# Hymba decoder layer on one core: K22 and KT4 activations in a right-hand pool of their own, the up product's pool 32 KiB lower

## The chip, the cores and the metric

The kernel runs on 1 core of one Trainium2 chip. The metric is the device time of one execution in microseconds; lower is better. Three executions of the kernel before took 2115.16, 2113.25 and 2115.39 us (median 2115.16). The profile comes from one more execution, which took 2114.84 us.

## What is computed

One decoder layer for 512 positions of width 2048 (float32): RMSNorm, an input projection, eight attention heads beside a 16-head SSM scan, an output projection added to x, and then the part that this change touches, the ConvGLU:

```python
x = x + jnp.concatenate([attn, ssm], axis=-1) @ w_out
h = rms_norm(x, norm2_w)
u = causal_dwconv(h @ w_up, ffn_conv_w, ffn_conv_b)
u_gate, u_val = jnp.split(u, 2, axis=-1)
return x + (jax.nn.silu(u_gate) * u_val) @ w_down
```

`w_up` is 2048 x 11264, `w_down` 5632 x 2048.

## The kernel before

**Two stages.** The first stage (to about 800 us) does everything up to and with the output projection, with helper functions whose instructions all stand under line 183. The second stage does the up and the down product. This change touches the second stage alone.

**The second stage.** Both products are done block by block with a 2 x 2 scheme of seven products (Strassen-Winograd): four weight quarters and four activation quarters are combined by sums into seven weight blocks and seven *kinds* of activations, `KT1, KT3, K11, KT2, K21, K22, KT4` (numbers 0 to 6, line 61). `groups` (lines 978 to 988) lists 44 groups of the up product and then 3 x 8 groups of the down product (passes over 7, 8 and 7 pairs of hidden blocks). Each group has seven items, `P1` to `P7`; `KIND` (line 63) says which kind each item uses: `P3` uses K22, `P4` uses KT4. Lines 997 to 999 set the order: P5 of a group, P3 of the group before, P1, P4 of the group before, P6, P2, P7.

**One item** ("slot") is lines 1285 to 1290: for each of n blocks (8 in the up product and the second pass, 7 in the first and third) two matmuls with the high half of the weights (`hi2`) against the high and the low half of the kind, and after them n matmuls with the low half of the weights (`lo2`) against the high half of the kind. So the weights of every matmul come from `hi2` or `lo2`, the moving operand (128 x 256) from a kind's tile `cmb0` to `cmb6`:

```python
pe.matmul(out, w, bk[:, 0, q, :], ...)
pe.matmul(out, w, bk[:, 1, q, :], ...)
...
pe.matmul(out, l[:, q * 128:(q + 1) * 128], bk[:, 0, q, :], ...)
```

The matmuls with the low half stand under line 1289 and are shown by the trace as one run of eight (or seven) per item.

**What feeds it.** SP loads the weights into `rawa` and `rawb`; DVE and POOL make the weight sums (lines 1013 to 1030); ACT makes `hi2` (line 1041) and DVE `lo2` (line 1050) some slots ahead. After an item, DVE or ACT takes its result out of PSUM (`up_after`, `down_after`). `events` and `after` hold what is issued at each slot; each engine works in the order of issue. The activations of a down pass come back from DRAM through `ld` tiles and are split into the kinds by `b_split` (lines 1096, 1097).

**Where tiles lie.** Pools are stacked from both ends of each partition's memory. From the near end: the constants, then, once the first stage's pools `w` and `ab` are closed, the pool `w2` (`lp`, line 970): `par2`, `rawb` x2, `rawa` x4, `acc_s` x2, `hi2` x3, `lo2` x2, and last `cmb5` (K22) and `cmb6` (KT4). From the far end: the pool `cmb` with `cmb0` to `cmb4`, written by `g_x2` during the output projection (lines 915 to 920), then `work2` (`xin` x5, `gx` x2, `sq`), which is closed at the start of the up product, and in its place the pool `up` (`ug`, `uv`, `ld`, `cP`, `tg`, `tv`, `gt`; line 1239), later `down`. A kind is 2 x 8 x 256 x 4 = 16,384 bytes per partition. By the order of allocation the bytes of each partition are:

| tile | bytes before | bytes after |
|---|---|---|
| first stage: `hi`, `lo` (weights) | 33,952 to 46,624 | same |
| first stage: `A`, `B` | 46,624 to 112,160 | same |
| first stage: `PTh`, `PTl`, `vh`, `vl` (attention) | 180,192 to 196,576 | same |
| `hi2`, `lo2` | 55,840 to 76,320 | same |
| `cmb5` (K22) | 76,320 to 92,704 | 114,656 to 131,040 |
| `cmb6` (KT4) | 92,704 to 109,088 | 131,040 to 147,424 |
| `up` | 110,432 to 147,424 | 77,664 to 114,656 |
| `work2` | 118,752 to 147,424 | same |
| `cmb0` to `cmb4` | 147,424 to 229,344 | same |

**The start of the up product.** K22 and KT4 are not made by `g_x2`. It stores their sums to DRAM (`xd`, line 921); `start_up` (line 1236) issues the first three `x_load`s, and `x_split` at the slots 2, 4, 5 and 6 (lines 1126 to 1136) writes K22 and KT4 from the `ld` tiles with ACT (line 1131) and DVE (line 1132). `P3` of the first group is slot 6, `P4` slot 8. A tile in a pool with `reuse_waits="tile"` waits for the last users of the older tiles that lay in its place.

Of the kernel before, what the change touches and what calls it, by code (L numbers as in the profile page):

```python
# [60 lines left out]
KT1, KT3, K11, KT2, K21, K22, KT4 = range(7)  # L61
# [126 lines left out]
def body(ctx, tc, xT, wi, wz, wo, wu, wd0, wd1, wd2, pp, pf, outT, dbg={}):  # L188
# [659 lines left out]
    p2 = {}  # L848

    def phase2():  # L850
        while gens:
            advance(True)
        work.close()
        cw.close()
        p2["cmb"] = ctx.enter_context(tc.tile_pool(name="cmb", bufs=1, side="right"))
        p2["kinds"] = [None] * 7
        for t in (KT1, KT3, K11, KT2, K21):
            p2["kinds"][t] = cmb_tile(t)
        p2["pool"] = work.enter_context(tc.tile_pool(name="work2", bufs=1, side="right"))
        p2["ssq"] = rbc  # L860

    def cmb_tile(t):

        pool = p2["cmb"] if t < K22 else p2["cmbl"]
        return pool.tile([128, 2, 8, 256], F32R, name="cmb%d" % t)

    x2d = [dram.tile([128, S], F32, name="x2d%d" % j) for j in range(NK)]
# [100 lines left out]
    ab.close()  # L968
    ve, se, pe, po, sy = nc.vector, nc.scalar, nc.tensor, nc.gpsimd, nc.sync
    lp = ctx.enter_context(tc.tile_pool(name="w2", bufs=1, reuse_waits="tile"))  # L970
    p2["cmbl"] = lp
    p2["par"] = lp.tile([128, NPF], F32, name="par2")
    sy.dma_start(p2["par"], pf)
    def side_tile(pool, shape, name, bufs=1):
# [113 lines left out]
    def b_split(k):  # L1088
        p, t, h = b_list[k]
        ph = [g for g in groups if g["ph"] == "down" and g["p"] == p][0]["kinds"]  # L1090
        m = PASSES[p][1] - 4 if h else 4
        if h == 0:
            ph[t] = cmb_tile(t)
        ld = lds.pop(0)
        hi, lo = (ph[t][:, x, 4 * h:4 * h + m, :] for x in range(2))
        se.activation(hi, ld[:, :m, :], AF.Copy)
        ve.tensor_tensor(lo, ld[:, :m, :], hi.bitcast(F32), op=OP.subtract)  # L1097
# [23 lines left out]
    def x_load(n):  # L1121
        if n < 4:
            x_ld.append(side_tile(box["pool"], [4, 256], "ld", 3))
            sy.dma_start(x_ld[n], xd[:, 4 * (n % 2):4 * (n % 2) + 4, n // 2, :])

    def x_split(n):
        t, h = (K22, KT4)[n // 2], n % 2
        if h == 0:
            up_kinds[t] = cmb_tile(t)
        o = up_kinds[t][:, :, 4 * h:4 * h + 4, :]  # L1130
        se.activation(o[:, 0], x_ld[n], AF.Copy)
        ve.tensor_tensor(o[:, 1], x_ld[n], o[:, 0].bitcast(F32), op=OP.subtract)
        x_load(n + 3)
# [102 lines left out]
    def start_up():  # L1236

        work.close()
        box["pool"] = up_stack.enter_context(tc.tile_pool(name="up", bufs=1, side="right", reuse_waits="tile"))
        box["depth"] = 3  # L1240
        for n in ("ug0", "uv0", "ug1", "uv1"):
            box[n] = box["pool"].tile([128, 516], F32, name=n)
            ve.memset(box[n][:, 0:2], 0.0)
        x_load(0), x_load(1), x_load(2)
# [21 lines left out]
    while gens:  # L1266
# [3 lines left out]
                                               reuse_waits="tile"))  # L1270
    step_slot(-2), step_slot(-1)
    for k, (gi, x) in enumerate(items):
        g = groups[gi]
        if x == "P5":
            g["X"] = box["ps"].tile([128, 512], F32, name="x")
        if x == "P2":
            g["Y"] = box["ps"].tile([128, 512], F32, name="y")
        out = g["Y"][:, :256] if x == "P2" else g["X"][:, 256:] if x in ("P5", "P3") else g["X"][:, :256]
        h, l = parts.pop(k)
        bk = g["kinds"][KIND[x]]  # L1280
        n = g["n"]
        fresh = x in ("P5", "P2")
        for part in ((range(n - 1), range(n - 1, n)) if k < 2 else (range(n),)):
            for q in part:
                w = h[:, q * 128:(q + 1) * 128]
                pe.matmul(out, w, bk[:, 0, q, :], start=fresh and q == 0, stop=False, skip_group_check=True)  # L1286
                pe.matmul(out, w, bk[:, 1, q, :], start=False, stop=False, skip_group_check=True)  # L1287
            for q in part:
                pe.matmul(out, l[:, q * 128:(q + 1) * 128], bk[:, 0, q, :], start=False, stop=q == n - 1,  # L1289
                          skip_group_check=True)  # L1290
        if k == 0:
            start_up()
        (up_after if g["ph"] == "up" else down_after)(g, x)
        step_slot(k)
# [23 lines left out]
```

## Time and profile before

| | |
|---|---|
| median of 3 executions | 2115.16 us (2113.25 to 2115.39) |
| the profiled execution | 2114.84 us |
| its span, first to last instruction | 2113.1 us |
| PE busy | 2073.9 us (98%) |
| DVE busy | 1583.5 us (75%) |
| ACT busy | 988.3 us (47%) |
| mean share of the DMA engines that is busy, second stage | some 40 to 80% |
| granted TensorE clock, mean | 0.998 |

The table stands for one profiled execution. PE is the bound of nearly the whole kernel, so a change is read from how closely its matmuls follow one another, and from the few places where it waits. In the chain of waits a run of matmuls of one line is merged into one piece, with its start, its length and its count; the distance between the starts of two such pieces is the time of one item.

### The profile page before, as it was taken

What the parts mean: (1) busy time and instruction counts of PE and PEld (TensorE: products, weight loads), DVE (VectorE), ACT (ScalarE), POOL (GpSimd) and SP (SyncE); (2) the same over time, 40 slices, a digit from 0 to 9 for tenths busy, and PEclk for the clock granted to TensorE, in tenths of its full rate; (3) what the DMA queues carried; (4) which work ended last, traced back from release to release, by engine and by line L of the source; (5) the groups of instructions that cost most, each with busy time, mean ns of one, the idle gap of its engine ahead of it and who ended that gap; (6) DMA issues with size and microseconds to landing.
All of it is one profiled execution on the core that took longest, in us unless ns stands there. A gap on an engine that the chain in (4) does not pass through costs nothing.

```text
span 2113.1 us, 37694 instructions
## 1 busy us (share of the span) xinstructions
PE 2073.9 (98%) x15366; PEld 1949.7 (92%) x15366; DVE 1583.5 (75%) x2251; ACT 988.3 (47%) x1433; POOL 207.9 (10%) x107
## 2 busy tenths in 40 slices
PE   9999999999999998999999999999999899999999
PEld 7888887888888878999999999999999899899999
DVE  6545555345555558999999999999999977977976
ACT  5433435244344435555555555555555534534532
POOL 0020000000000001111110111011111111101110
PEclk9999999999999999999999999999999999999999
DMA  5233222332225535445444444454455667856763
GB/s 194 75 115 91 71 75 76 99 101 80 80 70 172 165 129 188 158 141 189 160 156 165 170 168 155 157 183 158 142 188 201 215 215 242 274 184 231 260 201 120
DMA packets 114396, 328.18 MB, mean 155 GB/s; under 512 B 10736, under 2 KB 35120, under 8 KB 111408
## 3 DMA queue, kind: packets, MB, share of 16 engines
q1 hardware_dynamic: 114224, 325.78, 45.5%
q8 instruction: 120, 1.97, 0.4%
q14 instruction: 52, 0.43, 0.1%
HBM read 283.77 MB, written 41.98 MB: 154 GB/s over the span
## 4 chain that ended last, share of the span: by engine, by line
PE 88%; DVE 7%; issue 2%; ACT 1%; DMA 1%; SPq 0%; DVEq 0%; POOL 0%; ACTq 0%; POOLq 0%
PE acc L183 29%; PE x L1289 16%; PE x L1286 16%; PE x L1287 16%; PE sm L183 4%; PE y L1289 3%; PE y L1287 3%; PE y L1286 3%; DVE lo L1050 2%; DVE cmb L1097 1%; DVE lo L183 1%; DVE acc L1151 0%; DVE s L1024 0%; DMA raw<-wi 0%; DVE s L1030 0%
## 5 line engine op out<-in xcount | busy, mean ns | idle before, releaser
L1287 PE MATMUL x<-cmb,hi 128*128 128x256 f32 x3168 | 755.0, 279 | 12.5 <-DVE cmb L1097 10.9
L1286 PE MATMUL x<-cmb,hi 128*128 128x256 f32 x3168 | 755.8, 279 | 11.5 <-ACT cP L1166 5.4
L1287 PEld LDWEIGHTS x<-cmb,hi 128*128 128x128 f32 x3168 | 599.3, 189 | 15.2 <-DVE cmb L1097 13.4
L1286 PEld LDWEIGHTS x<-cmb,hi 128*128 128x128 f32 x3168 | 598.7, 189 | 13.4 <-issue 7.5
L1289 PE MATMUL x<-cmb,lo 128*128 128x256 f32 x3168 | 434.3, 279 | 2.6 <-DVE lo L1050 2.6
L1289 PEld LDWEIGHTS x<-cmb,lo 128*128 128x128 f32 x3168 | 397.2, 189 | 3.6 <-DVE lo L1050 3.4
L183 DVE TENSOR_TENSOR lo<-raw,hi 128x512 fp32r<-128x512 f32 (+1 forms) x240 | 164.4, 691 | 243.0 <-ACT hi L183 228.5
L1041 ACT ACTIVATE hi<-s 128x1024 fp32r<-128x1024 f32 (+1 forms) x201 | 201.0, 1000 | 287.3 <-DVE s L1024 192.2
L1017 POOL TENSOR_TENSOR rawb<-rawa,rawb 128x1024 f32<-128x1024 f32 (+1 forms) x68 | 169.7, 2496 | 1308.1 <-DVE s L1024 1070.8
L183 PE MATMUL acc<-A,hi 128*128 128x512 f32 x704 | 281.5, 400 | 0.5 <-ACT hi L183 0.5
L183 PE MATMUL acc<-A,lo 128*128 128x512 f32 x704 | 277.9, 395 | 0.1
L183 PE MATMUL acc<-B,hi 128*128 128x512 f32 x704 | 276.8, 393 | 0.0
L183 ACT ACTIVATE hi<-raw 128x512 fp32r<-128x512 f32 (+1 forms) x240 | 149.6, 629 | 256.2 <-PE acc L183 220.3
L1050 DVE TENSOR_TENSOR lo<-s,hi 128x1024 fp32r<-128x1024 f32 (+1 forms) x201 | 238.6, 1187 | 18.8 <-issue 18.8
L1050 DVE TENSOR_TENSOR lo<-rawa,hi 128x1024 fp32r<-128x1024 f32 (+1 forms) x204 | 242.0, 1186 | 3.6 <-PE x L1289 3.6
L1041 ACT ACTIVATE hi<-rawa 128x1024 fp32r<-128x1024 f32 (+1 forms) x204 | 209.5, 1028 | 40.0 <-PE x L1287 39.9
L183 PEld LDWEIGHTS acc<-A,lo 128*128 128x128 f32 x704 | 132.1, 188 | 33.0 <-DVE lo L183 2.1
L183 PEld LDWEIGHTS acc<-A,hi 128*128 128x128 f32 x704 | 132.7, 188 | 29.5 <-ACT hi L183 1.8
L183 PEld LDWEIGHTS acc<-B,hi 128*128 128x128 f32 x704 | 132.5, 188 | 28.3
L1166 ACT ACTIVATE cP<-x 128x256 f32<-128x256 f32 x132 | 50.9, 385 | 214.0 <-PE x L1289 214.0
L183 PE MATMUL acc<-hi,A 128*128 128x256 f32 (+2 forms) x448 | 135.4, 302 | 0.7 <-DVE u L183 0.7
L183 PE MATMUL acc<-lo,A 128*128 128x256 f32 (+2 forms) x448 | 133.5, 298 | 0.0
(204 smaller groups left out, 2777.2 us busy)
## 6 DMA issues: line engine op xcount, KB each, us to landing
rawa<-wu SPq DMA_DIRECT2D x176, 512.0 KB, 3.6
raw<-wi SPq DMA_DIRECT2D x79, 512.0 KB, 3.6
rawa<-wd SPq DMA_DIRECT2D x64, 448.0 KB, 4.1
rawb<-wu SPq DMA_DIRECT2D x44, 512.0 KB, 4.5
gd<-gt SPq DMA_DIRECT2D x22, 1024.0 KB, 4.6
raw<-wo SPq DMA_DIRECT2D x32, 512.0 KB, 3.6
rawa<-wd SPq DMA_DIRECT2D x32, 512.0 KB, 4.4
ld<-gd SPq DMA_DIRECT2D x27, 512.0 KB, 6.4
```

Of the source, the lines that this page charges most:

```text
L183: return fn(out, *args, **kw)
L1017: po.tensor_tensor(r, raw[gi, "11"][:, :n], r, op=OP.subtract)
L1041: se.activation(h[:, :n], src[:, :n], AF.Copy)
L1050: ve.tensor_tensor(l[:, :n], src[:, :n], h[:, :n].bitcast(F32), op=OP.subtract)
L1097: ve.tensor_tensor(lo, ld[:, :m, :], hi.bitcast(F32), op=OP.subtract)
L1166: se.activation(g[x], X[:, 256:] if x == "P5" else X[:, :256], AF.Copy)
L1286: pe.matmul(out, w, bk[:, 0, q, :], start=fresh and q == 0, stop=False, skip_group_check=True)
L1287: pe.matmul(out, w, bk[:, 1, q, :], start=False, stop=False, skip_group_check=True)
L1289: pe.matmul(out, l[:, q * 128:(q + 1) * 128], bk[:, 0, q, :], start=False, stop=q == n - 1, skip_group_check=True)
```

## The change

The two last kinds get a pool of their own, `cmb2`, on the right side. It is opened in `start_up`, when `work2` is closed and before `up` is opened. `w2` loses the 32 KiB of these two kinds, which were last in it, and `up` (and `down` after it) lies 32 KiB lower. No instruction is added, removed or reordered.

```diff
     def cmb_tile(t):
 
-        pool = p2["cmb"] if t < K22 else p2["cmbl"]
+        pool = p2["cmb"] if t < K22 else p2["cmb2"]
         return pool.tile([128, 2, 8, 256], F32R, name="cmb%d" % t)
...
     lp = ctx.enter_context(tc.tile_pool(name="w2", bufs=1, reuse_waits="tile"))
-    p2["cmbl"] = lp
     p2["par"] = lp.tile([128, NPF], F32, name="par2")
...
     def start_up():
 
         work.close()
+        p2["cmb2"] = ctx.enter_context(tc.tile_pool(name="cmb2", bufs=1, side="right", reuse_waits="tile"))
         box["pool"] = up_stack.enter_context(tc.tile_pool(name="up", bufs=1, side="right", reuse_waits="tile"))
```

## Rows read from the trace of the kernel before

**Rows 1.** The page: busy time of each engine, and the chain that ended last, by engine.

```profile
PE 2073.9 (98%) x15366; PEld 1949.7 (92%) x15366; DVE 1583.5 (75%) x2251; ACT 988.3 (47%) x1433; POOL 207.9 (10%) x107
...
PE 88%; DVE 7%; issue 2%; ACT 1%; DMA 1%; SPq 0%; DVEq 0%; POOL 0%; ACTq 0%; POOLq 0%
```

**Rows 2.** Chain of waits, one group of the up product: start, length, what.

```profile
1001.60 0.96 PE x L1289 x8
...
1009.83 0.91 PE x L1289 x8
1012.55 0.91 PE x L1289 x8
1015.36 0.96 PE x L1289 x8
1018.15 0.91 PE x L1289 x8
1020.96 0.96 PE x L1289 x8
```

**Rows 3.** Timeline of PE in the first stage, one attention product: start, length, operation.

```profile
646.11 0.28 PE L183 MATMUL sm<-PTh,vl 128*128 128x256 f32 x1
646.23 0.28 PE L183 MATMUL sm<-PTh,vh 128*128 128x256 f32 x1
646.35 0.28 PE L183 MATMUL sm<-PTl,vh 128*128 128x256 f32 x1
```

**Rows 4.** Chain of waits, one group of the first down pass, then of the second.

```profile
1726.40 0.84 PE x L1289 x7
...
1728.84 0.79 PE x L1289 x7
1731.22 0.79 PE y L1289 x7
...
1743.34 0.84 PE x L1289 x7
...
1851.04 0.96 PE x L1289 x8
...
1870.40 0.96 PE x L1289 x8
```

**Rows 5.** By window: its length; busy PE, PEld, DVE, ACT, POOL; clock, DMA, GB/s.

```profile
1001.60:1040.32 38.72, 38.72 (x338) 38.72 (x338) 36.15 (x46) 20.14 (x26) 4.92 (x2) 1.00 0.45 163
1649.00:1707.00 58.00, 46.56 (x364) 44.49 (x363) 54.66 (x72) 30.31 (x37) 7.94 (x3) 0.97 0.74 254
1802.00:1838.00 36.00, 31.57 (x260) 30.26 (x259) 35.59 (x40) 23.25 (x25) 5.81 (x2) 1.00 0.88 302
1962.00:1994.00 32.00, 29.16 (x241) 28.16 (x240) 32.00 (x40) 20.62 (x24) 4.46 (x2) 1.00 0.87 297
```

**Rows 6.** Timelines of SP, DVE and ACT at the start of the up product.

```profile
796.68 0.38 SPq L921 DMA_DIRECT2D xd<-gx  x1
799.60 2.30 SPq L1124 DMA_DIRECT2D ld<-xd  x3
...
797.77 0.69 DVE L183 TENSOR_TENSOR rbc<-rbc,sq 128x512 f32<-128x512 f32 x1
...
809.25 1.05 ACT L1131 ACTIVATE cmb<-ld 128x1024 fp32r<-128x1024 f32 x1
810.20 1.02 ACT L1041 ACTIVATE hi<-s 128x1024 fp32r<-128x1024 f32 x1
```

**Rows 7.** DMA issues, median us to landing (last column).

```profile
xd<-gx SPq DMA_DIRECT2D x8, 256.0 KB, 2.7
```

**Rows 8.** Groups of instructions: busy, mean ns | idle before.

```profile
L1050 DVE TENSOR_TENSOR lo<-rawa,hi 128x1024 fp32r<-128x1024 f32 x156 | 189.9, 1218 | 3.6 <-PE x L1289 3.6
...
L1097 DVE TENSOR_TENSOR cmb<-ld,cmb 128x1024 fp32r<-128x1024 f32 x27 | 33.0, 1229 | 0.0
```

**Rows 9.** Timelines of DVE and PE around one P5 item.

```profile
1009.52 1.22 DVE L1050 TENSOR_TENSOR lo<-s,hi 128x1024 fp32r<-128x1024 f32 x1
...
1012.39 1.07 PE L1289 MATMUL x<-cmb,lo 128*128 128x256 f32 x8
```

## The prediction

> **What bounds the kernel now.** I read the page first: PE is busy for 98% of the span and makes up 88% of the chain that ended last; no other engine has more than 7% of that chain [rows 1]. So time can be won only where matmuls follow each other faster, or where PE waits. Next I read the chain of waits in a quiet stretch of the up product, for the distance between the eight-matmul runs of line 1289, which is the time of an item [rows 2]. The run under result y is P2, and the order of items names the others: the run at 1001.60 is P4, then come P6, P2, P7 (1009.83), P5 (1012.55), P3 (1015.36), P1 (1018.15) and P4 again (1020.96). From P7 to P5 is 2.72 us. All runs take 0.91 us, 0.114 us a matmul, but those of P3 and P4 take 0.96, 0.120 a matmul. These two are the items whose moving operand is K22 or KT4. [...] What sets the two apart is the place: their moving operand lies below byte 109,088, on the same side as all weights (55,840 to 76,320), while `cmb0` to `cmb4` begin at 147,424.
>
> Is it the place, then, or the item? The first stage has a test. In the attention products the moving operand (`PTh`, `PTl`) and the weights (`vh`, `vl`) both lie above byte 180,192, and they follow at 0.12 us for the same 256 columns [rows 3]. So 0.12 comes with both operands on one side, near or far, and 0.114 with the operands on different sides. That is the working theory: a matmul that streams from one side while the next weights are read from the same side pays some 6 ns.
>
> **The sum, part by part.** *K22 and KT4 move to the far side.* A group takes 1020.96 - 1001.60 = 19.36 us [rows 2]; seven items at 2.72 make 19.04. So the near side costs 0.32 us a group, and the whole of it lies on the chain. A group of the first down pass (seven blocks) takes 1743.34 - 1726.40 = 16.94 us, with fast items of 1731.22 - 1728.84 = 2.38; seven of these are 16.66, so 0.28 a group. The second pass has 1870.40 - 1851.04 = 19.36, again 0.32 [rows 4]. The third has the blocks of the first, 0.28. Over 44 + 8 + 8 + 8 groups that is 44 x 0.32 + 8 x 0.28 + 8 x 0.32 + 8 x 0.28 = 21.1 us.
>
> Not all of it arrives. At the start of each down pass DVE is the bound: busy 54.66 of 58 us, 35.59 of 36 and 32.00 of 32, and PE waits there [rows 5]. A faster matmul only waits longer. P3 and P4 of the last up group, of groups 1, 2 and 8 of the first pass, of 1 and 8 of the second and of 1 of the third fall into these stretches: 4 x 0.28 + 3 x 0.32 = 2.1 us. What of this is lost is between nothing and all; I take all, because DVE has hardly an idle microsecond in those rows. The term is 21.1 - 2.1 = 19.0 us.
>
> *Can the others follow?* In the quiet stretch DVE is busy 36.15 of 38.72 us for two groups, ACT 20.14 [rows 5]. After the change two groups would take 38.08, so DVE still idles 1.9 us. The tightest item is P5: its low half is ready at 1009.52 + 1.22 = 1010.74, its run begins at 1012.39 [rows 9], 1.65 us of slack, of which a group that is 0.32 us shorter can take at most 0.32. So DVE does not become the bound in the quiet stretches, and I cost this at nothing; without that cover the gain would end at DVE's 18.1 us a group, below the 19.04 wanted.
>
> *`w2` shrinks.* The two kinds were its last tiles, so its other tiles stay: nothing.
>
> *The waits of the new pool.* K22 and KT4 now lie where `work2` was. Their first write, by ACT at 809.25, must wait for the last users of `xin`, `gx` and `sq`: the sum that reads `sq` ends at 798.46, and the store of `xd`, issued at 796.68, lands about 2.7 us later, near 799.4 [rows 6, 7]. Both are ten microseconds early, so nothing. If that cover were gone, ACT would stand at line 1131 with the next `hi2` of line 1041 (810.20) queued behind it, and PE behind that. In exchange the first load from `xd` no longer waits for users of `xin`; it could go up to 799.60 - 797.06 = 2.5 us sooner, but its data is used at 809.25, so that is nothing too. SP's order, and the number of DMAs and of instructions, stay as they are.
>
> *`up` and `down` lie 32 KiB lower.* Their tiles are used by DVE, ACT and DMA alone. The bound for DVE: 1024 elements with everything near take 1218 ns (line 1050), with `ld` and mostly far kinds 1229 (line 1097) [rows 8]. Eleven nanoseconds either way, over some 15 such widths (36.15 / 2 us by 1.218), is 0.2 us of DVE's 1.3 us idle: nothing on the chain. Whether they disturb PE's weight reads is a rival below.
>
> The sum against the profiled execution is 2114.84 - 19.0 = **2095.8 us**. That execution lies 0.3 us under the median of the runs shown, and it has 1.7 us outside its span that I leave alone. A measurement of this kernel can tell about 0.2% (4.2 us) from no change.
>
> **The rivals.** *Only KT4 gets across (2105.3 us).* The last near tile in use is `B`, up to byte 112,160, and the first far one `cmb0`, from 147,424; where between these one side ends no row shows. K22's new place, 114,656 to 131,040, and KT4's, 131,040 to 147,424, fill just this gap. If the sides are equal halves of what the program fills (229,344 bytes, middle 114,672), K22 is across, and KT4 too. If the border is near KT4's start, P3 stays at 0.96 and P4 falls to 0.91; half the term is 9.5 us: 2114.84 - 9.5 = 2105.3. For it: nothing in the trace excludes it, and K22 starts right at the middle. Against it: it needs unequal sides. [...]
>
> *It is the item, not the place (2114.8 us, the same).* P3 and P4 are also the only items that belong to the group before, and add to its PSUM tile while the next group is under way. Then nothing changes; nor would it if the far side began only at 147,424. Against it: the attention rows have 0.12 without any such order [rows 3], and a run of 0.96 is even throughout. [...]
>
> *The near side becomes crowded (slower, about 2154 us).* `up`'s whole traffic moves to the side from which all weights are read. If reads by DVE and ACT there slow the weight reads as the moving operand does, every item becomes a slow one: 24 x 0.006 = 0.14 us more than 2.72, a group 20.0 instead of 19.36, or 0.66 us more; with 52 such groups and 16 of seven blocks (some 0.6) that is 44 us, and with the seven DVE-bound groups left out 39 us: 2154. It decides from 0.32 / 7 = 0.046 us an item, above which it eats the whole gain. Against it: `rawa`, `hi2` and `lo2` already make the near side the busier one for DVE and ACT, and the pieces of the other five items are 0.91 all the same, whatever DVE does beside them [rows 2, 9].
>
> **How the numbers follow.** Both kinds across 0.50; KT4 alone 0.35; item or border beyond 147,424, the same, 0.09; crowded 0.06. The point is the likeliest case, 2095.8. Its own range is 2093 (all 21.1 arrive, and some scatter) to 2098. Two cases together hold 0.85, so the range for 8 in 10 must reach the second: 2093 to 2107. Faster by over 0.2%: 0.50 + 0.35 = 0.85; within 0.2%: 0.09; slower: 0.06.
>
> **What would show it.** Right: in a quiet group all seven runs take 0.91 and a group 19.04; the first pass has 16.66 a group; DVE's busy time per group is unchanged, its idle time smaller; ACT's first write of K22 has no wait. P3 at 0.96 with P4 at 0.91 and 19.20 a group is the first rival, both at 0.96 the second, all seven at 0.96 the third. The forecast is wrong if a quiet group is not 19.04, or if the down passes lose what the up product wins because DVE runs late there over more than the three stretches named.

## The result and the profile after

The changed kernel takes **2127.99 us** (median of 6 runs, 2125.38 to 2130.94) against 2113.60 (6 runs, 2112.28 to 2115.39): a ratio of 1.0067 with the interval 1.0054 to 1.0080. It is slower, by 14 us, where 19 us less were forecast. Busy time and the chain of the page of after, against [rows 1]:

```profile
PE 2087.9 (98%) x15366; PEld 1965.4 (92%) x15366; DVE 1583.9 (74%) x2251; ACT 988.3 (46%) x1433; POOL 208.1 (10%) x107
...
PE 90%; DVE 7%; issue 1%; DMA 1%; ACT 1%; SPq 0%; DVEq 0%; POOL 0%; ACTq 0%; POOLq 0%
```

All 14 us are PE's (2073.9 before); the others have the same busy time and PE the same number of instructions. The chain of waits of after, in the stretch of [rows 2] (start, length, what):

```profile
1003.55 0.94 PE x L1289 x8
...
1006.38 0.94 PE x L1289 x8
...
1009.21 0.94 PE y L1289 x8
...
1023.34 0.94 PE x L1289 x8
```

The first and the last line are P4 of two groups: 19.79 us, before it was 19.36. P3 and P4 no longer stand out. But all seven items are now alike at 2.83 us, 0.118 a matmul, which is neither of the values of [rows 2]: P3 and P4 gained, the other five lost. Next the same view in the first down pass, then in the second, then in the third [rows 4]:

```profile
1730.42 0.82 PE y L1289 x7
1732.89 0.82 PE x L1289 x7
...
1747.73 0.82 PE y L1289 x7
...
1871.52 0.91 PE x L1289 x8
...
1890.56 0.91 PE x L1289 x8
...
2047.58 0.79 PE y L1289 x7
2049.96 0.79 PE x L1289 x7
```

The first pass has the slow pace too: 17.31 us a group (16.94 before). The second has 19.04, and the third 2.38 an item: exactly the forecast, P3 and P4 with the rest. So **one kernel has two paces in one execution**: 0.118 in the up product and in the first pass, 0.113 in the other two, but for some items beside the waits at the ends and starts of the stages. I call them the slow and the quick rhythm. In the trace's own records of after, a matmul starts 110 ns after the load of its weights begins in the quick rhythm (1871 to 1890 us), and the starts are 113, 113, 114 ns apart; in the slow one (1003 to 1043 us) it is 114 to 115 ns, and 117 to 119 apart.

The kernel before has both too, which its quiet groups don't show. In its up product, from 810 us to the first P3, matmuls start 117 to 119 ns apart but for the waits; right behind that P3 they are 113 to 114 apart. These are runs of line 1289 of P5, of that P3, and of P6 a little later (timeline of PE, before):

```profile
818.26 1.10 PE L1289 MATMUL x<-cmb,lo 128*128 128x256 f32 x8
821.11 1.12 PE L1289 MATMUL x<-cmb,lo 128*128 128x256 f32 x8
...
829.99 1.07 PE L1289 MATMUL x<-cmb,lo 128*128 128x256 f32 x8
```

Where the time went is read from one item, a P2, at four places (chain of waits, before):

```profile
871.59 0.91 PE y L1289 x8
...
1714.28 0.79 PE y L1289 x7
...
1842.79 0.91 PE y L1289 x8
...
2100.05 0.79 PE y L1289 x7
```

The same four items in after:

```profile
870.70 0.94 PE y L1289 x8
...
1730.42 0.82 PE y L1289 x7
...
1860.64 0.91 PE y L1289 x8
...
2114.22 0.79 PE y L1289 x7
```

After is 0.89 us ahead at the first, 16.14 behind at the second, 17.85 at the third and 14.17 at the last. The up product lost 17.0 us (about 40 groups by 0.43), the first pass 1.7; the second and third won 3.7. No new wait is needed for this sum. The windows of after, against [rows 5] (length; busy PE, PEld, DVE, ACT, POOL; clock, DMA, GB/s), show the same clock in a quiet stretch, and DVE's work in it unchanged:

```profile
1003.55:1043.14 39.59, 39.59 (x339) 39.59 (x338) 36.24 (x46) 20.13 (x26) 4.93 (x2) 1.00 0.46 160
```

### The profile page after: what moved, and what is told of

It reads as the page before. It is cut to its first block, busy times and chain, and to the rows that moved or that the text cites. A ratio compares the mean times of both kernels' runs of the same rounds, so it can differ in the third digit from the quotient of the medians.

```text
span 2127.1 us, 37695 instructions
## 1 busy us (share of the span) xinstructions
PE 2087.9 (98%) x15366; PEld 1965.4 (92%) x15366; DVE 1583.9 (74%) x2251; ACT 988.3 (46%) x1433; POOL 208.1 (10%) x107
## 4 chain that ended last, share of the span: by engine, by line
PE 90%; DVE 7%; issue 1%; DMA 1%; ACT 1%; SPq 0%; DVEq 0%; POOL 0%; ACTq 0%; POOLq 0%
PE acc L183 30%; PE x L1287 16%; PE x L1286 16%; PE x L1289 16%; PE sm L183 4%; PE y L1286 3%; PE y L1289 3%; PE y L1287 3%; DVE lo L1049 1%; DVE cmb L1096 1%; DVE acc L1150 0%; DVE lo L183 0%; DVE s L1023 0%; DVE s L1027 0%; DMA acc<-x2d 0%
```

## The experiments

Below, the **distance** of an item is the byte address of its weights (`hi2`, `lo2`) less that of its activations, as a remainder by 512. It is the same for all matmuls of an item, as the blocks within both lie whole multiples of 512 apart. Before, it is 55,840 - 76,320 = -20,480, that is 0, for K22, and 0 for KT4; 55,840 - 147,424 = -91,584, that is 64, for `cmb0` to `cmb4`. The change puts all seven kinds at 64. So it altered two things at once: the side, and the low bits of the address.

**One kind alone** (`e1`: only K22 goes to `cmb2`; `e2`: only KT4).

```diff
-        pool = p2["cmb"] if t < K22 else p2["cmb2"]
+        pool = p2["cmb"] if t < K22 else p2["cmb2"] if t == K22 else p2["cmbl"]
...
+    p2["cmbl"] = lp
```

> K22 alone in the far pool, KT4 left in its old place on the near side; up lies 16 KiB lower. Theory 1 (two rhythms: with operands on different sides a matmul can follow at 0.113 or at 0.118 us, an item with both operands on one side costs 0.120 but always hands on the short rhythm): in the up product P4 runs in 0.96, all others in 0.91, a group takes 19.20 us, and the time is about half of the forecast gain below the kernel before, some 2104 us. Theory 2 (the near side is crowded by the tiles of up, which now lie there for the greater part): the items other than P4 take 0.93 or 0.94 in the up product, a group 19.6 to 19.8, the time is 2114 us or more.

> KT4 alone in the far pool, K22 left near. Theory 1: the mirror image of the run with K22 alone: P3 0.96, the others 0.91, a group 19.20 us, some 2104 us. Theory 2: other items 0.93 to 0.94, a group 19.6 to 19.8, 2114 us or more.

Measured: e1 2104.84 us (ratio 0.9954, interval 0.9940 to 0.9968), e2 2104.95 (0.9955, 0.9941 to 0.9969). Each kind is worth half of the forecast when it moves alone, and the loss comes only when both move. The chain of e1 at the start of the up product suggests why:

```profile
823.24 0.94 PE x L1290 x8
...
826.09 0.96 PE x L1290 x8
...
828.88 0.91 PE x L1290 x8
...
842.48 0.91 PE x L1290 x8
845.29 0.96 PE x L1290 x8
```

The up product begins in the slow rhythm (0.94). Then comes a P4, whose kind is still at distance 0 (0.96), and behind it the other items are quick (0.91), as they still are from 1001 to 1042 us. So the reading is that a P4 at 0.120 does not only cost its own 0.16 us; the items behind it run at 0.113 *because of it*. In the kernel before, P3 and P4 would do this in every group, and with both moved nothing would do it any more. One change of pace behind one P4 does not prove that; the runs that set the rhythm by hand, below, test it.

**Near side, other low bits** (`e3`: the kernel before, with K22 and KT4 left on the near side, but 448 bytes further on, so that their distance is 64).

```diff
             if t == K22:
+                lp.tile([128, 112], F32, name="pad")
```

> The kernel before with K22 and KT4 still near, but 448 bytes further on, so that they stand to the weights modulo 512 bytes as the far kinds do. If the side decides: P3 and P4 stay at 0.96, a group at 19.36, the time at 2114 us. If the low bits of the addresses decide (same distance modulo 512 costs): P3 and P4 lose their 0.96, and the time is that of the changed kernel (2128) or of the forecast (2096).

Its four runs fall into two kinds, so that their median (2111.87 us) says little: 2096.22 and 2097.92 us, and 2125.81 and 2133.61, the one with the profile (chain of waits):

```profile
1001.18 0.94 PE x L1291 x8
...
1004.00 0.94 PE x L1291 x8
...
1009.66 0.94 PE y L1291 x8
```

The y run is P2, the one at 1004.00 P4. P4 has no price of its own here (0.94, as P2 has) although its operand lies on the near side, beside the weights. This points away from the side as what costs 0.120; `e13` below repeats it with the rhythm held. The times also put the same kernel in either rhythm from one execution to the next: some 30 us lie between the pairs, as much as 40 groups of 19.79 and 19.04 differ by. That is an estimate, as only the slow rhythm has a profile here. The granted clock does not set the pairs apart (0.998 in the execution shown, 0.996 to 0.998 in the others).

**Far side, other low bits** (`e5` to `e10`: the kernel after with a pad ahead of `hi2`, which shifts `hi2` and `lo2` alone; seven kinds on the far side throughout).

```diff
+        if k == 0:
+            lp.tile([128, 112], F32, name="pad")
         h = lp.tile([128, 1024], F32R, name="hi2", bufs=3)
```

> The kernel after, with hi2 and lo2 moved 448 bytes further, so that in all seven kinds the weights start a whole multiple of 512 bytes from the activations, while all seven kinds still lie on the other side of the partition from them. Theory of the low bits: every run of eight matmuls takes 0.96 us in up as P3 and P4 did before (0.120 each), a group of up lasts 7 x 2.88 = 20.2 us in place of 19.79, and all four passes are at this pace in every execution: 2128 + 24 x 0.37 + 24 x 1.1 (second pass, up and down not alike) is about 2150 to 2160. Theory of the side: other side means 0.91 or 0.94 as in the kernel after, 2096 to 2131.

> The same, with hi2 and lo2 moved by 64 bytes in place of 448: the distance is 128 past a multiple of 512 in all kinds. Theory of the low bits: no item at 0.120; each pass falls into one of the two rhythms (0.113 or 0.118 a matmul), 2096 to 2131, unless this distance allows only one of them, which the spread of the runs would show (below 1 us). Theory of the side: the same as the kernel after, 2125 to 2131, since nothing changes sides.

> The same with 192 bytes: distance 256 past a multiple of 512. Theory of the low bits: either the two rhythms (2096 to 2131), or, if 256 counts as aligned too, 0.120 throughout, 2150 to 2160. Theory of the side: 2125 to 2131.

> The same with 320 bytes: distance 384 past a multiple of 512. Theory of the low bits: the two rhythms or one of them, 2096 to 2131. Theory of the side: 2125 to 2131.

> The kernel after, with hi2 and lo2 moved by 32 bytes: the distance from weights to activations is 96 past a multiple of 512 in all kinds. So far 0 and 256 gave 0.120 throughout (2161), 128 and 384 0.1186 (2148.5), 64 the two rhythms 0.1133 and 0.1178 (2098 to 2131). If only whole multiples of 128 cost, it is the two rhythms again, 2096 to 2131 with some 5 us between runs; if nearness to a multiple of 128 costs, something between, 2131 to 2148; if this distance allows the quick rhythm alone, 2094 to 2097 with under 2 us between runs.

> The same with 480 bytes: distance 32 past a multiple of 512. If only whole multiples of 128 cost: 2096 to 2131, as e9. If nearness to a multiple of 256 costs: 2131 to 2161. If the quick rhythm alone: 2094 to 2097.

| run | distance of all seven kinds | us, median (range) | ratio to before | item of up, profiled execution, us |
|---|---|---|---|---|
| after | 64 | 2127.99 (2125.38 to 2130.94) | 1.0067 | 2.83 |
| e10 | 32 | 2144.04 (2143.37 to 2146.63) | 1.0142 | 2.84 |
| e9 | 96 | 2137.33 (2132.40 to 2148.46) | 1.0115 | 2.85 |
| e6 | 128 | 2148.93 (2147.18 to 2149.34) | 1.0166 | 2.85 |
| e8 | 384 | 2148.12 (2146.66 to 2149.58) | 1.0163 | 2.85 |
| e7 | 256 | 2160.93 (2159.95 to 2163.41) | 1.0226 | 2.88 |
| e5 | 0 | 2161.20 (2160.58 to 2161.53) | 1.0225 | 2.88 |

The chain of waits of e5:

```profile
1005.95 0.96 PE x L1291 x8
1008.83 0.96 PE x L1291 x8
1011.71 0.96 PE x L1291 x8
```

With every kind on the far side, P3 and P4's old price is on all seven items as soon as the distance is 0 (2.88 an item), and 256 gives the same. This settles it from one end (0.96 across the sides), and e3 with e13 from the other (0.94 and 0.91 on one side): in these runs the 0.120 goes with the low bits of the distance, whichever side the operands are on. 128 and 384 lie between; there I had expected the two rhythms and 2096 to 2131 us, which missed by some 17. Since 0 and 256 are alike, and 128 and 384, a remainder by 256 would serve these runs as well. At 32 and 96 I had put down the quick rhythm alone, the two rhythms, or something slower; it was the last, and from 1004 to 1017 us the profiled executions have 0.95 a run, none 0.91. At 96 that is said of one execution, the slowest: the other three were 10 to 16 us shorter and have no trace. In these stretches of the up product only the distance 64 showed the quick rhythm (0.91 in e11 and e13 below). The pace changed within one kernel at another distance too; e6 has 0.95 here in its up product and 0.96 in its second pass:

```profile
1003.12 0.95 PE x L1291 x8
...
1903.92 0.96 PE x L1291 x8
```

**Setting the rhythm by hand.** If a stretch at 0.120 hands on the quick rhythm, a short one will do, once behind the stalls at the start of each stage. `e4` has one of 24 matmuls, in the up product only; `e11` four of eight matmuls; I call such a short run a kick. Weights and moving operand are both `hi2`, distance 0, and what they write is overwritten by the item's own first matmul. `e12` is the control, the same with the item's activations (distance 64).

```diff
+        if (gi, x) in ((2, "P5"), (47, "P5"), (54, "P5"), (62, "P5")):
+            for _ in range(8):
+                pe.matmul(out, h[:, :128], h[:, :256], start=True, stop=True, skip_group_check=True)
```

> The changed kernel with 24 extra matmuls once, before P5 of the fourth up group, with both operands from hi2, so both on the near side; their result is overwritten by P5. Theory 1: groups before it take 19.79 us, the groups after it 19.04 until the first down pass, 40 groups x 0.75 = 30 us less and 2.9 us for the extra matmuls: about 2101 us. Theory 2: nothing but 2.9 us more, 2131 us, all groups 19.79.

> The kernel after, with four short runs of eight extra matmuls whose moving operand is hi2 itself (distance from the weights a whole multiple of 512), behind the stalls at the start of up and of each down pass; their output is overwritten. Theory that a stretch at 0.120 hands on the quick rhythm, whichever was there: every item behind each is 2720 in up and the second pass and 2380 in the other two, in every execution; 4 x 0.96 is 3.8 us on top of 2095: 2097 to 2100, under 2 us between runs. Theory that the rhythm is only drawn by the stall: the runs spread as in the kernel after, 2100 to 2135.

> Control: the same four runs of eight extra matmuls at the same places, with the moving operand of the item itself (distance 64). Theory that a stretch at 0.120 sets the rhythm: these change nothing but their own 3.7 us, so the passes are drawn as in the kernel after, some at 2827 or 2473, 2115 to 2135 in most runs. Theory that any break in the order of the work sets it: 2097 to 2100 as e11.

e4 took 2103.04 us (2098.43 to 2107.74, ratio 0.9945, interval 0.9928 to 0.9963), but is no proof by itself. In its profiled execution the quick rhythm was there before the extra matmuls, behind a stall in the second group (run of 1.11 us, chain of waits):

```profile
821.09 0.94 PE x L1292 x8
823.92 1.11 PE x L1292 x8
826.85 0.91 PE x L1292 x8
```

e11 took **2099.40 us** (2098.49 to 2100.35, ratio 0.9927, interval 0.9911 to 0.9944), its control 2133.50 (2130.20 to 2139.80, ratio 1.0093, 1.0071 to 1.0116). The chain of e11 around its first kick (line 1285):

```profile
832.81 0.94 PE y L1292 x8
...
835.64 0.94 PE x L1292 x8
836.58 0.95 PE x L1285 x8
...
839.36 0.91 PE x L1292 x8
```

And of the control:

```profile
832.69 0.94 PE y L1292 x8
...
835.51 0.94 PE x L1292 x8
836.46 0.94 PE x L1285 x8
...
839.28 0.94 PE x L1292 x8
```

Slow before and quick behind the kick at distance 0 (0.94, then 0.91); slow on both sides of the same kick at distance 64 (0.94). The four runs of e11 lie within 2 us. The spans of the two profiled executions are 2098.6 and 2128.5 us, 29.9 apart; the up product alone, 40 groups by 19.79 - 19.04, makes 30.0 of that, so by this estimate the down passes of the two took about the same time.

**The side again, with the rhythm held, and two more.** `e13` is e3 with the four kicks of e11, `e14` the kernel before with these kicks, and `e15` is e11 with two matmuls a kick in place of eight.

> The kernel before with K22 and KT4 left on the near side, only 448 bytes further on (distance 64, as in e3), and the four kicks of e11 to hold the rhythm fixed. Theory of the low bits alone: the same as e11, 2097 to 2101 in every run, groups of 19.04 and 16.66 with P3 and P4 at 0.91 and 0.79. If the near side has a price of its own beside the low bits (P3 and P4 above 0.91): 2105 to 2116.

> The kernel before, nothing moved, with the four kicks of e11. If P3 and P4 at 0.120 already hand on the quick rhythm to the rest of each group, the kicks have nothing to mend and cost their own 4 x 0.96: 2117 to 2120 against 2114. If the kernel before also loses time to the slow rhythm: 2112 or less.

> The kernel after with kicks of two matmuls in place of eight. If the first matmul at 0.120 already breaks the slow rhythm: 2096 to 2098 in every run, quick items behind each kick. If the rhythm needs a longer stretch to be lost: runs spread as in the kernel after, 2100 to 2135, with 2827 behind some kick.

e13 took 2099.47 us (2098.03 to 2101.24, ratio 0.9928, interval 0.9912 to 0.9943), the same as e11. Its chain, from P3 at 1012.46 and P4 at 1017.90, both with near activations, to P2:

```profile
1012.46 0.91 PE x L1294 x8
...
1017.90 0.91 PE x L1294 x8
...
1023.34 0.91 PE y L1294 x8
```

So the side has no price that these runs can see: 448 bytes of padding do what the new pool does. e14 took 2116.96 us (ratio 1.0013, 1.0004 to 1.0023), about 3 us more than before and about the kicks' own 4 x 0.94: before, P3 and P4 leave a kick nothing to mend, as the reading of e1 has it. e15 took 2106.02 (2100.72 to 2108.19, ratio 0.9954, 0.9939 to 0.9969). Two matmuls disturbed the rhythm, but did not set it. In the profiled execution the kick in the up product turned slow into quick (runs of 0.94 at 835.35 us, of 0.91 at 838.36), the one in the first pass quick into slow (chain of waits, kick at 1704.34):

```profile
1701.17 0.79 PE y L1292 x7
1703.55 0.79 PE x L1292 x7
1704.34 0.23 PE x L1285 x2
...
1706.22 0.82 PE x L1292 x7
```

## Why the prediction was wrong

**The cause of 0.120 was misread.** "What sets the two apart is the place" is right as far as it goes: in the quiet stretch PE is busy throughout at a granted clock of 1.00 [rows 5], and all its matmuls there stream 128x256, so that wait, clock and shape are the same for P3 and P4 as for the rest. But of the place I took the side and left out the low bits. P3 and P4 differed from the others in both, and so did the rows that I used as a test: `PTh` and `vh` of [rows 3] lie on one side, and their addresses too differ by a whole multiple of 512. The test could not tell the two apart; e3, e5 and e13 do. Since the change moves the kinds from distance 0 to 64, this error alone would have cost nothing: their own 0.120 did go, as in both the second and third pass.

**The step that failed** is "seven items at 2.72 make 19.04". It takes 2.72 as what an item with far activations costs. But 2.72 was one of two paces that such an item can have, and in the kernel before it was P3 and P4, the items to be mended, that kept the others on it. With them gone the up product stays at 2.83: a group of 19.79, and the term that should have been -0.32 a group is +0.43. Where the quick rhythm came by chance or by a kick, the step holds to the hundredth: the second and third pass of after, and the up product of e11 and e13 from 1002 us (19.04 a group). e11 less its four kicks (2099.4 - 3.8) is 2095.6, against the 2095.8 of the forecast; that it comes within 0.2 us is in part luck, as its runs spread over 2 us, and the items ahead of its kick in the up product are slow (0.94). The 2.1 us that the prediction wrote off at the starts of the passes were not measured by themselves. Why after enters the slow rhythm at the start of up in each of its runs (the 30 us between the rhythms in that stage, 40 x 0.75, would show in their 6 us spread), while e3 and e4 sometimes left it, was not settled. Nor does any run show what inside PE makes the two paces; shown is what brings one or the other. The trace of the kernel before had the sign: the slow pace ahead of its first P3 (117 to 119 ns), at a distance of 64.

**The other steps held.** PE waits for the same things for as long as before. The longest group of PE's waits of after (line, what it waited for: us in total, times, longest):

```profile
PE x L1287 <- DVE cmb L1096: 11.1, 12, 2.3
```

Before, it stood at 10.9 us. DVE could follow where PE was quick: the groups of e11 and e13 last 19.04 from 1002 us on. The first write of K22 waited for nothing of the new pool: ACT begins it right behind `cP`, and what ACT waited for was PE (timeline of ACT in after; in brackets the idle time before and what ended it).

```profile
808.16 0.38 ACT L1165 ACTIVATE cP<-x 128x256 f32<-128x256 f32 x1 [2.16 <-PE x L1289]
808.44 1.05 ACT L1130 ACTIVATE cmb<-ld 128x1024 fp32r<-128x1024 f32 x1
```

DVE's operations with `up` on the near side take what they took: the low half of `rawa` 1214 ns, the sum into `cmb` 1214 (1218 and 1229 in [rows 8]).

**The rivals.** KT4 alone across is out: after shows P3 and P4 alike everywhere, and e1 and e2 are worth the same. That the item matters and not the place is out by e1 and e2. The crowded near side, the only rival on the slower side, is out although the kernel did get slower: with `down` on the near side too, the second and third pass have 0.91 and 0.79, and e11 has 0.91 with `up` there. It asked for 0.96 on all seven and 2154 us; that picture came only from the distance, in e5. None of the rivals was the one that decided, a pace that the slow items themselves set for the rest, and the range of 2093 to 2107 had no room for it.

## What to carry to other kernels

When two groups of operands differ in speed, write down all that differs in their addresses, the low bits as well as the region, and look for a row in which these come apart before giving the price to one. And don't take the pace of the quicker items for their own as long as others run between them: change one of the two alone first, as e1 does; had only that been tried, both would have looked like sure gains. In this kernel, with the change, eight extra matmuls in each of four places were worth 34 us (e11 against its control) or 29 (against after); in the kernel before they cost 3 (e14). The change and the kicks together are 15 us below before.

## What the runs showed that I had not expected

- Equal matmuls with fp32 operands ran at 0.118 us each for some 850 us (after, 812 to 1669 us, runs of 0.94) and at 0.113 for some 140 us (after, 1854 to 1994 us, runs of 0.91) of one execution, at one granted clock (1.00). Which of the two comes behind a stall was open: behind the run of 1.11 us e4 was quick (0.91), behind the stalls that end near 1723 us and 1854 us after was slow (0.82) and quick (0.91).
- The pace went with the distance between weights and moving operand: in the stretches profiled 0.120 at 0 and 256, 0.119 at 128 and 384 (0.120 later on in e6) and, in one execution, at 96, 0.118 at 32, 0.113 or 0.118 at 64.
- Eight matmuls at distance 0 turned the slow pace into the quick one where it was shown (e11, 0.94 ahead of the kick in the up product and 0.91 behind it), and the eight runs of e11 and e13 lie between 2098.03 and 2101.24 us. In e4 the quick pace came behind a stall. Behind two such matmuls (e15) the up product was quick (0.91) and the first pass slow (0.82).
- The best version found keeps the change and adds the four kicks (e11, 2099.4 us), and the kernel before with 448 bytes of padding and the same kicks does as well (e13, 2099.5).
